# Order of the last two gate blocks in a half, three small jobs on other engines, and two queue intervals, in a two-layer hybrid encoder

## The chip, the cores and the metric

The kernel runs on one core of one Trainium2 chip. The metric is the time of one execution on the device in microseconds (us). A core has five engines with an instruction stream each: TensorE (PE in the profile; its weight loads are PEld) multiplies matrices into PSUM, VectorE (DVE), ScalarE (ACT) and GpSimd (POOL) do elementwise work, and SyncE (SP) issues DMAs. Each engine takes its instructions in order, so that an instruction that waits holds up all that stand behind it on its engine.

## What is computed

The reference runs two layers over 2048 rows (tokens) of 1024 values in float32:

```
for l in range(DEPTH):                                 # DEPTH = 2
    h = rmsnorm(x, pre_g[l])
    proj = jnp.einsum('bsd,de->bse', h, w_in[l])
    u_a, v_a, g_a, q, k, v, g_b = jnp.split(proj, idx, axis=-1)   # 512, 512, 512, 512, 128, 128, 512
    y_a = gmlp_group(u_a, v_a, ln_a_g[l], ln_a_b[l], spatial_w[l], spatial_b[l]) * jax.nn.silu(g_a)
    y_b = gqa_axial_attention(q, k, v, q_norm_g[l], k_norm_g[l], tables) * jax.nn.silu(g_b)
    out = jnp.einsum('bse,ed->bsd', jnp.concatenate([y_a, y_b], axis=-1), w_out[l])
    x = x + rmsnorm(out, post_g[l])
```

`gmlp_group` normalises v over its channels, mixes it over the 128 rows of a chunk with one 128x128 matrix per group of 64 channels, adds a bias per row, and multiplies by u. `gqa_axial_attention` has 8 query heads and 2 key/value heads of 64, with normalised and rotated q and k, and attends over all 2048 rows.

## The kernel before

**Number format.** Most products are made in three passes of a high and a low part (`PASSES`: high times high, high times low, low times high). A weight block of 256 columns is loaded as `w_raw` (`load_w`), and `split_w` makes `w_hi` (a ScalarE copy, L267) and `w_lo` (a VectorE subtraction, L268) from it. Seven buffers hold such blocks.

**Projections.** `Project.run` handles the 2048 rows in two halves, each of two groups of 512 rows. A group's rows are loaded (`x_t`), normalised (squares on ScalarE, a reciprocal root in eight small VectorE steps, and a scaling by `g_row` on VectorE, L299), transposed on TensorE, and stored as high and low part `hT` (a ScalarE copy, L309, and a VectorE subtraction, L310). `hT_jobs` returns this work as four `preps` (rows) and eight `trans` (a half row tile each). Within a half the blocks of columns come in the order k/v, q (two blocks), v of the gating part (two blocks together), attention gate (two blocks, `do_gb`), and then four gate blocks c = 0 to 3, each with 128 gate columns and 128 u columns: for each group 24 matmuls for the gate (`proj_ch`), 24 for u, and `do_gate`. In the first half, just before the product of the last gate block with the second group, the `preps` of the next half's first group are called, and its `trans` are handed to `bg`. The tiles `hT` of a group, `k_t`, `v_t` and later `wo` share six buffers ("big"), so that the next half's `hT` takes the buffers of the first group of this half when that group's last product is done.

**What sets the order.** `bg` is a list of jobs with due times, counted in ticks: `proj_ch` ticks after every 4 of its 24 matmuls, `proj_tok` after every 8, and each tick runs at most two due jobs. `bg.flush()` at the end of a half runs what is left, all at once. Instructions that are made through `PE`, `ACT`, `DVE` and `POOL` (all of TensorE's among them; they all carry line L84 in the profile) stay in the order of the program. Those made through `nc.scalar`, `nc.vector`, `nc.gpsimd` and `nc.sync` are sorted by the framework, which places an instruction where it believes its engine to be free and its inputs and buffers to be ready, sometimes far ahead of its place in the program.

**Small jobs that the change touches.** `norm_row` loads `g_row` (128x1024) and multiplies it by a constant on ScalarE (L185); layer 0 does so at the start, and for layer 1 it is called at the start of layer 0's attention. `spatial_weights` (called in the first half of each layer) transposes the eight mixing matrices, copies them from PSUM to `wsT` on VectorE (L233, two of 128x512), and makes `zbias` with eight VectorE copies of 64x128 from PSUM (L249, L250). A fill with ones of two partitions of `k_t` (2x4096 halves, L1187, VectorE) stands at the beginning of each layer; the rows are needed from the attention on.

**Attention.** `attend` makes 32 units (4 blocks of 512 queries, 8 heads) of 16 steps, with one step k of the loop for each 128 keys: two score matmuls (`sp`), two exponentials on ScalarE, a subtraction (GpSimd, every seventh on VectorE), and the products of earlier steps (`po`, `sums`). Other work is put into the steps by number: 16 steps with the row maxima of a later unit (`pmax` on TensorE, a VectorE reduction `mx`), `max_row` (`m_neg`), and `stack_max`, which transposes `m_neg` on TensorE (`t`) and stores it for `load_q` of that unit, at step `k0 + span + 3`, two after `max_row`. The output projection of the query block before (`pout`) fills in between. The steps that follow a finished output tile (`post_steps`: eight small VectorE steps of a reciprocal root, two VectorE additions of 128x512, a store, and in layer 0 for the first eight tiles also the next layer's normalisation with two more 128x512 scalings, 24 steps in all) go to `post_queue`, of which each k takes at most two. For the last four tiles of a layer (`last=True`) `post_steps` begins with four multiplications by `g_post` of 128x256 on GpSimd (`gain`); the steps of two tiles are interleaved.

Of the kernel before, what the change touches and what calls it, by code (L numbers as in the profile page):

```python
# [14 lines left out]
ALU = mybir.AluOpType  # L15
# [4 lines left out]
P = 128  # L20
# [3 lines left out]
TPG = GRP // P  # L24
NH = 8
HD = 64
# [8 lines left out]
NORM_SCALE = -8192.0 / D ** 0.5  # L35
# [3 lines left out]
def encoder(ctx: ExitStack, tc, x, w_in, w_out, pre_g, post_g, ln_a_g, ln_a_b,  # L39
            spatial_w, spatial_b, q_norm_g, k_norm_g, rope, out):  # L40
    nc = tc.nc
# [133 lines left out]
    class Project:  # L175
# [5 lines left out]
        def norm_row(self):  # L181

            self.g_row = lay.tile([P, D], F32, name="g_row")
            nc.sync.dma_start(self.g_row, pre_g[self.l].partition_broadcast(P))
            nc.scalar.mul(self.g_row, self.g_row, 1.0 / NORM_SCALE)  # L185

# [28 lines left out]
        def spatial_weights(self):  # L215
# [5 lines left out]
            for hf in range(2):  # L221
# [6 lines left out]
                def t(hf=hf, raw=raw, hi=hi, lo=lo):  # L228
# [3 lines left out]
                    sl = slice(hf * GRP, (hf + 1) * GRP)  # L232
                    nc.vector.tensor_copy(wsT[:, sl], ps)  # L233
                    nc.scalar.copy(hi, wsT[:, sl])
# [8 lines left out]
            for c in range(4):  # L243
                def b(c=c):
# [3 lines left out]
                    PE.matmul(ps[:, 0:2 * P], ones1, sb[:, 2 * c * P:(2 * c + 2) * P], start=False, stop=True)  # L248
                    nc.vector.tensor_copy(self.zbias[0:HD, c, :], ps[0:HD, 0:P])  # L249
                    nc.vector.tensor_copy(self.zbias[HD:P, c, :], ps[HD:P, P:2 * P])  # L250
                bg.add(WS_DELAY + 8 + 2 * c, b)
# [269 lines left out]
        def run(self, kv, first, last_jobs, first_wo):  # L521
# [5 lines left out]
            for n, gs in enumerate(halves):  # L527
# [50 lines left out]
                if n + 1 < len(halves):  # L578
                    blocks.append([C_K])
                if n + 1 == len(halves):  # L580
                    self.scale_v()
                    last_jobs()
                for b in range(2):
# [5 lines left out]
                    w = w_next  # L589
                for c in range(4):  # L590
                    raw = self.load_w(blocks.pop(0)) if blocks else None
                    for i, g in enumerate(gs):
                        if i == len(gs) - 1 and c == 3 and n + 1 < len(halves):
                            g2 = halves[n + 1][0]
                            hTs[g2], preps, trans = self.hT_jobs(g2)
                            for j in range(TPG):
                                preps[j]()
                            for m, f in enumerate(trans):
                                bg.add(6 + 2 * m, f)
                        pg = self.proj_ch(hTs[g], w, 0)  # L600
                        pu = self.proj_ch(hTs[g], w, P)
                        self.do_gate(g, c, pg, pu)
                        if i == 0 and c == 3 and n + 1 == len(halves):
                            hTs[g] = None
                            first_wo()
                        if i == 0 and raw is not None:
                            w_next = self.split_w(raw)
                    w = w_next
                w_kv = w
# [19 lines left out]
    def attend(l, kv, nxt):  # L629
# [25 lines left out]
        def at(k, f):  # L655
            later.setdefault(k, []).append(f)
# [298 lines left out]
        def post_steps(s, t, last=False):  # L955
            z = small.tile([P, 1], F32, name="rs_o", bufs=4)

            def gain(i):
                sl = slice(i * WB, (i + 1) * WB)
                return lambda: POOL.tensor_tensor(s.o[:, sl], s.o[:, sl], g_post[:, sl], ALU.mult)  # L960

# [82 lines left out]
        for u in range(pre, len(units)):  # L1044
# [5 lines left out]
            at(k0 + span + 1, lambda u=u: max_row(u, DVE))  # L1050
            at(k0 + span + 3, lambda u=u: stack_max(u, PE, ACT, DVE))

# [39 lines left out]
        for k in range(end + 4):  # L1092
            if k < total:
# [11 lines left out]
                if not dve_share(k):  # L1105
                    sub_lo(k, POOL)
            for _ in range(2):
                if post_queue:
                    post_queue.pop(0)()
            kb = k - 1  # L1110
# [70 lines left out]
    for l in range(DEPTH):  # L1181
# [4 lines left out]
        kv.append(v_t.bitcast(F16)[:, 1].rearrange("p (t k d) -> p t k d", t=NT, k=NKV))  # L1186
        nc.vector.memset(kv[1][HD:HD + 2], 1.0)  # L1187
        att = attend(l, kv, layers[l + 1] if l + 1 < DEPTH else None)
# [43 lines left out]
```

## Time and profile before

| | us |
|---|---|
| median of 3 runs | 2773.86 (2772.46 to 2774.44) |
| the profiled execution: its time | 2771.47 |
| the profiled execution: span from first to last instruction | 2769.3 |
| TensorE busy | 2677.1 (97%) |
| VectorE busy | 1896.8 (68%) |
| ScalarE busy | 1522.7 (55%) |
| GpSimd busy | 1287.0 (46%) |

The first layer's projections take the first 620 us of the span or so, its attention lasts to about 1390, and the second layer follows in the same way. A row of a timeline has the start, the duration, engine, line, operation, output and inputs, shapes and a count where several of a kind follow one another; in brackets is the idle time of the engine before it, and what ended that. A row of the waits view has who waited for whom, the total in us, how many times, and the longest. A row of the windows view has a stretch and its length, the busy time of each engine with its count of instructions, then TensorE's granted clock as a share, the mean share of the DMA engines, and GB/s.

### The profile page before, as it was taken

How to read it: one execution, taken by the hardware profiler on the slowest of the kernel's cores; microseconds unless marked ns; L12 is line 12 of the kernel's file. 1: busy time of each engine (PE TensorE's matmuls, PEld its weight loads, DVE VectorE, ACT ScalarE, POOL GpSimd, SP SyncE). 2: the span in 40 equal slices, each digit the busy share in tenths (PEclk: the TensorE clock that was granted, in tenths of full speed). 3: DMA queues.
4: the chain of work that ended last, by engine and by line, in shares of the span. 5: the costliest groups of instructions: out<-in, count | busy, mean ns of one | idle time of the engine just before them, and what ended most of it. 6: DMA issues, size and time to landing. Idle time of an engine off the chain costs nothing.

```text
span 2769.3 us, 48428 instructions
## 1 busy us (share of the span) xinstructions
PE 2677.1 (97%) x18230; PEld 1782.0 (64%) x18230; DVE 1896.8 (68%) x3796; ACT 1522.7 (55%) x3005; POOL 1287.0 (46%) x1080
## 2 busy tenths in 40 slices
PE   7999999999999999999999999999999999999997
PEld 6898899764444444444589989997644444444444
DVE  8862688876666776776487528888766666666664
ACT  4221432117887787787732214221288877778774
POOL 1210122007786676776632101210277767667765
PEclk9999999999999999999999999999999999999999
DMA  4424522322222232222354334333322222221313
GB/s 143 146 81 127 165 76 81 112 63 89 89 71 81 75 98 79 82 80 80 110 179 138 115 114 134 88 92 98 94 64 72 82 70 73 81 76 47 112 46 129
DMA packets 275310, 265.31 MB, mean 96 GB/s; under 512 B 19202, under 2 KB 233346, under 8 KB 275076
## 3 DMA queue, kind: packets, MB, share of 16 engines
q1 hardware_dynamic: 275076, 262.22, 30.2%
q8 instruction: 143, 2.34, 0.3%
q14 instruction: 91, 0.75, 0.1%
HBM read 177.09 MB, written 85.07 MB: 95 GB/s over the span
## 4 chain that ended last, share of the span: by engine, by line
PE 77%; DVE 11%; ACT 5%; DMA 3%; issue 2%; POOL 1%; SPq 0%; DVEq 0%; POOLq 0%; ACTq 0%
PE pp L84 27%; PE sp L84 14%; PE po L84 11%; PE pout L84 11%; PE pmax L84 7%; PE sums L84 4%; PE pt L84 2%; DVE fc L363 2%; ACT p_parts L84 2%; ACT p_f L84 2%; DMA w_raw<-in_w_in_dram 1%; DVE mx L84 1%; DVE o_t L84 1%; DVE w_lo L268 1%; ACT w_hi L267 1%
## 5 line engine op out<-in xcount | busy, mean ns | idle before, releaser
L84 POOL TENSOR_TENSOR p_parts<-p_f,p_parts 128x512 f16<-128x512 f32 x872 | 1034.9, 1205 | 404.2 <-ACT p_f L84 304.3
L84 ACT ACTIVATE p_parts<-sp 128x512 f16<-128x512 f32 x1024 | 630.0, 615 | 296.5 <-PE sp L84 289.8
L84 DVE TENSOR_REDUCE mx<-pmax 128x1 f32<-128x512 f32 x768 | 513.0, 681 | 211.9 <-PE pmax L84 209.9
L84 PE MATMUL pout<-wo,y_t 128*128 128x512 f32 x1488 | 657.1, 506 | 0.7 <-ACT p_f L84 0.3
L84 PE MATMUL po<-p_parts,v_st 128*32 128x512 f16 (+1 forms) x3072 | 639.2, 383 | 0.2
L84 ACT ACTIVATE p_f<-sp 128x512 f32<-128x512 f32 x1024 | 632.0, 617 | 0.0
L84 PE MATMUL pp<-w_hi,hT 128*128 128x256 f32 x3584 | 502.5, 290 | 16.1 <-DVE hT L310 9.7
L84 PEld LDWEIGHTS pp<-w_hi,hT 128*128 128x128 f32 x3584 | 462.0, 194 | 21.8 <-DVE hT L310 10.9
L84 PE MATMUL sp<-q_st,k_t 128*128 128x512 f16 x1024 | 390.2, 381 | 8.3 <-DVE mx L84 5.5
L84 PE MATMUL pmax<-k_t,q_m 128*128 128x512 f16 x1024 | 389.7, 382 | 7.6 <-DVE mx L84 3.2
L84 PEld LDWEIGHTS <-v_st 128*32 128x32 f16 (+1 forms) x3072 | 193.7, 96 | 309.5 <-issue 253.0
L84 PE MATMUL sp<-q,k_t 66*128 66x512 f16 x1024 | 391.0, 382 | 0.0
L84 PEld LDWEIGHTS pout<-wo,y_t 128*128 128x128 f32 x1488 | 281.3, 190 | 128.4 <-issue 8.7
L84 PEld LDWEIGHTS <-k_t 128*128 128x128 f16 (+1 forms) x2048 | 191.5, 99 | 187.7 <-issue 74.4
L468 POOL TENSOR_TENSOR fl<-fa,fh 128x512 fp32r<-128x512 f32 x32 | 43.1, 1346 | 533.3 <-ACT fh L467 489.2
L84 PE MATMUL pp<-hT,w_hi 128*128 128x512 f32 x1024 | 271.7, 413 | 0.0
L84 PE MATMUL pp<-w_lo,hT 128*128 128x256 f32 x1792 | 262.6, 290 | 0.0
L84 PE MATMUL sums<-p_parts,one_h 128*32 128x512 f16 x2048 | 242.3, 380 | 0.0
L84 PEld LDWEIGHTS pp<-w_lo,hT 128*128 128x128 f32 x1792 | 235.5, 194 | 0.9
L84 PEld LDWEIGHTS pp<-hT,w_hi 128*128 128x128 f32 x1024 | 193.4, 190 | 35.3
L683 DVE TENSOR_REDUCE mx<-pmax 128x1 f32<-128x512 f32 x256 | 172.6, 687 | 49.1 <-PE pmax L84 47.5
L84 PEld LDWEIGHTS <-q_m 128*128 128x128 f16 x1024 | 99.8, 98 | 140.2 <-issue 42.1
(161 smaller groups left out, 2790.9 us busy)
## 6 DMA issues: line engine op xcount, KB each, us to landing
w_raw<-in_w_in_dram SPq DMA_DIRECT2D x28, 1024.0 KB
y_t<-y_d SPq DMA_DIRECT2D x56, 512.0 KB
w_raw<-in_w_in_dram SPq DMA_DIRECT2D x32, 512.0 KB
x_t<-in_x_dram SPq DMA_DIRECT2D x16, 512.0 KB
z_d<-fb SPq DMA_DIRECT2D x32, 256.0 KB
gb_d<-fa SPq DMA_DIRECT2D x32, 256.0 KB
fb<-z_d SPq DMA_DIRECT2D x32, 256.0 KB
y_d<-fh SPq DMA_DIRECT2D x32, 256.0 KB
```

The costliest lines, as they stand in the source:

```text
L84: return tc.keep_in_program_order(call(*args, **kw))
L267: nc.scalar.copy(hi[:, sl], raw[:, sl])
L268: nc.vector.tensor_tensor(lo[:, sl], raw[:, sl], hi.bitcast(F32)[:, sl], ALU.subtract)
L363: nc.vector.tensor_tensor(t2[:, :, :, lo:lo + 16], qn[:, :, :, hi:hi + 16], tbi[:, :, 1:2, lo:lo + 16].broadcast_to([P, 2, n, 16]), ALU.mult)
L468: nc.gpsimd.tensor_tensor(lo, th, hi.bitcast(F32), ALU.subtract)
L683: dve.tensor_reduce(s.mx[:, j, c:c + 1], ps, AX.X, ALU.max)
```

## The change

- In the first half of each layer, gate blocks 2 and 3 are made group by group: (block 2, group 0), (3, 0), (2, 1), (3, 1) in place of (2, 0), (2, 1), (3, 0), (3, 1). The `preps` and `trans` of the next half are started ahead of (2, 1), which is two products of a block with a group ahead of the end in place of one. Block 3 is split one product earlier. In both halves the next weight block is loaded right after the split of the one before.
- `g_row` is scaled on GpSimd in place of ScalarE.
- `wsT` and `zbias` are copied from PSUM by ScalarE in place of VectorE.
- The fill of ones is made by GpSimd in place of VectorE, and stands in the last half of each layer, ahead of `scale_v`.
- `gain` of the last tile of the last layer runs on VectorE in place of GpSimd.
- `stack_max` comes two steps later, and `post_queue` gives one piece per step in place of two.

```diff
-            nc.scalar.mul(self.g_row, self.g_row, 1.0 / NORM_SCALE)
+            nc.gpsimd.tensor_scalar(self.g_row, self.g_row, 1.0 / NORM_SCALE, None, ALU.mult)
...
-                    nc.vector.tensor_copy(wsT[:, sl], ps)
+                    nc.scalar.copy(wsT[:, sl], ps)
...
-                    nc.vector.tensor_copy(self.zbias[0:HD, c, :], ps[0:HD, 0:P])
-                    nc.vector.tensor_copy(self.zbias[HD:P, c, :], ps[HD:P, P:2 * P])
+                    nc.scalar.copy(self.zbias[0:HD, c, :], ps[0:HD, 0:P])
+                    nc.scalar.copy(self.zbias[HD:P, c, :], ps[HD:P, P:2 * P])
...
                 if n + 1 == len(halves):
+                    nc.gpsimd.memset(self.kv[1][HD:HD + 2], 1.0)
                     self.scale_v()
...
-                for c in range(4):
-                    raw = self.load_w(blocks.pop(0)) if blocks else None
-                    for i, g in enumerate(gs):
-                        if i == len(gs) - 1 and c == 3 and n + 1 < len(halves):
-                            g2 = halves[n + 1][0]
-                            hTs[g2], preps, trans = self.hT_jobs(g2)
-                            for j in range(TPG):
-                                preps[j]()
-                            for m, f in enumerate(trans):
-                                bg.add(6 + 2 * m, f)
-                        pg = self.proj_ch(hTs[g], w, 0)
-                        pu = self.proj_ch(hTs[g], w, P)
-                        self.do_gate(g, c, pg, pu)
...
-                        if i == 0 and raw is not None:
-                            w_next = self.split_w(raw)
-                    w = w_next
+                more = n + 1 < len(halves)
+                order = [(c, i) for c in range(4) for i in range(len(gs))]
+                if more:
+                    order[-2 * len(gs):] = [(c, i) for i in range(len(gs)) for c in (2, 3)]
+                parts, raw = {0: w}, self.load_w(blocks.pop(0))
+                for m, (c, i) in enumerate(order):
+                    g = gs[i]
+                    if more and (c, i) == (2, len(gs) - 1):
+                        g2 = halves[n + 1][0]
+                        hTs[g2], preps, trans = self.hT_jobs(g2)
+                        for j in range(TPG):
+                            preps[j]()
+                        for j, f in enumerate(trans):
+                            bg.add(6 + 2 * j, f)
+                    pg = self.proj_ch(hTs[g], parts[c], 0)
+                    pu = self.proj_ch(hTs[g], parts[c], P)
+                    self.do_gate(g, c, pg, pu)
...
+                    split = (len(parts) - 1) * len(gs)
+                    if more and len(parts) == 3:
+                        split -= 1
+                    if raw is not None and m >= split:
+                        parts[len(parts)] = self.split_w(raw)
+                        raw = self.load_w(blocks.pop(0)) if blocks else None
...
-                return lambda: POOL.tensor_tensor(s.o[:, sl], s.o[:, sl], g_post[:, sl], ALU.mult)
+                engine = DVE if nxt is None and t == NT - 1 else POOL
+                return lambda: engine.tensor_tensor(s.o[:, sl], s.o[:, sl], g_post[:, sl], ALU.mult)
...
-            at(k0 + span + 3, lambda u=u: stack_max(u, PE, ACT, DVE))
+            at(k0 + span + 5, lambda u=u: stack_max(u, PE, ACT, DVE))
...
-            for _ in range(2):
-                if post_queue:
-                    post_queue.pop(0)()
+            if post_queue:
+                post_queue.pop(0)()
...
-        nc.vector.memset(kv[1][HD:HD + 2], 1.0)
```

More of the change, by code (lines that the diff above doesn't have):

```diff
@@ L589, in run @@
                     w = w_next
-                for c in range(4):
-                    raw = self.load_w(blocks.pop(0)) if blocks else None
-                    for i, g in enumerate(gs):
-                        if i == len(gs) - 1 and c == 3 and n + 1 < len(halves):
-                            g2 = halves[n + 1][0]
-                            hTs[g2], preps, trans = self.hT_jobs(g2)
-                            for j in range(TPG):
-                                preps[j]()
-                            for m, f in enumerate(trans):
-                                bg.add(6 + 2 * m, f)
-                        pg = self.proj_ch(hTs[g], w, 0)
-                        pu = self.proj_ch(hTs[g], w, P)
-                        self.do_gate(g, c, pg, pu)
-                        if i == 0 and c == 3 and n + 1 == len(halves):
-                            hTs[g] = None
-                            first_wo()
-                        if i == 0 and raw is not None:
-                            w_next = self.split_w(raw)
-                    w = w_next
+                more = n + 1 < len(halves)
@@ new lines, in run @@
+                order = [(c, i) for c in range(4) for i in range(len(gs))]
[14 more added lines that the diff above has]
+                    self.do_gate(g, c, pg, pu)
+                    if not more and (c, i) == (3, 0):
+                        hTs[g] = None
+                        first_wo()
+                    split = (len(parts) - 1) * len(gs)
[4 more added lines that the diff above has]
+                        raw = self.load_w(blocks.pop(0)) if blocks else None
@@ L609, in run @@
+                w = parts[max(parts)]
                 w_kv = w
```

## The prediction

> **What bounds the kernel now.** I read the page first, then TensorE's waits, then short windows around the longest of them.
>
> ```profile
> span 2769.3 us, 48428 instructions
> ...
> PE 2677.1 (97%) x18230; PEld 1782.0 (64%) x18230; DVE 1896.8 (68%) x3796; ACT 1522.7 (55%) x3005; POOL 1287.0 (46%) x1080
> ```
>
> TensorE is busy for 2677.1 of 2769.3 us. The change leaves its matmuls as they are, so all that can be gained lies in its 92.2 idle us, and in time when it is busy but slow. Its waits, in the waits view of TensorE alone, name the places:
>
> ```profile
> PE pp L84 <- DVE hT L310: 9.7, 5, 4.6
> PE t L84 <- DVE m_neg L84: 6.3, 9, 1.1
> PE sp L84 <- DVE mx L84: 5.5, 6, 1.9
> PE pp L84 <- DVE zbias L250: 4.5, 2, 2.5
> PE pt L84 <- DVE hT L84: 4.5, 1, 4.5
> PE pt L84 <- DVE fc L365: 3.9, 4, 3.0
> PE pmax L84 <- DVE mx L84: 3.2, 3, 1.5
> ```
>
> These seven end on VectorE, each at a small job, and the change touches all but `fc`. Windows add a second cost:
>
> ```profile
> 123.20:126.50 3.30, 3.27 (x15) 3.30 (x16) 3.21 (x7) 0.00 (x0) 1.39 (x1) 0.50 0.99 353
> 320.00:330.00 10.00, 10.00 (x86) 10.00 (x85) 10.00 (x38) 4.79 (x15) 1.98 (x2) 1.00 0.68 221
> 956.00:959.40 3.40, 3.40 (x23) 1.24 (x25) 3.26 (x12) 2.35 (x5) 1.69 (x2) 0.50 0.20 81
> 1150.60:1153.90 3.30, 3.30 (x19) 1.22 (x22) 3.19 (x11) 2.32 (x5) 2.96 (x3) 0.50 0.20 81
> 1405.10:1409.90 4.80, 4.77 (x23) 4.77 (x24) 4.80 (x12) 0.59 (x1) 2.32 (x3) 0.50 0.14 47
> 1693.40:1696.60 3.20, 3.20 (x17) 3.20 (x16) 3.20 (x16) 2.62 (x8) 0.00 (x0) 0.50 0.92 307
> ```
>
> The third number from the end is the granted clock. Right behind five of the longest stalls TensorE runs for 3 to 5 us at 0.50: 15 matmuls in 3.30 us at 123, against 86 in 10 us at 320. Half of such a window is lost on top of the stall, yet it counts as busy.
>
> **Part by part.** The sum is made against the profiled execution's 2771.47 us (2.2 around its span), which is 2.4 under the median of 2773.86.
>
> *Order of the gate blocks.*
>
> ```profile
> 290.00:302.00 12.00, 12.00 (x55) 9.94 (x54) 7.33 (x16) 7.87 (x19) 1.50 (x1) 1.00 0.40 103
> 302.00:314.00 12.00, 12.00 (x61) 9.94 (x60) 11.54 (x35) 3.90 (x8) 1.29 (x1) 1.00 0.51 160
> 345.00:390.00 45.00, 44.27 (x371) 43.99 (x370) 38.94 (x96) 15.79 (x35) 9.60 (x9) 1.00 0.27 82
> ```
>
> ```profile
> 314.32 0.69 DVE L310 TENSOR_TENSOR hT<-pt,hT 128x512 fp32r<-128x512 f32 x1 [0.46 <-ACT hT L309]
> ...
> 314.85 2.35 PE L84 MATMUL pt<-ident,x_t 128*128 128x128 f32 x20
> 319.32 1.22 PE L84 MATMUL pp<-w_hi,hT 128*128 128x256 f32 x8 [2.13 <-DVE hT L310]
> ...
> 1691.69 1.22 PE L84 MATMUL pp<-w_hi,hT 128*128 128x256 f32 x8 [2.13 <-DVE hT L310]
> ```
>
> In a window's row VectorE is the third of the busy times (those with x and a count). A block has 48 matmuls and so 12 ticks; the eight transposes are due at ticks 6 to 20, so that three run in the last block and five (20 matmuls, 2.35 us) in the flush, whose evacuations TensorE then waits for: 2.13 us in each layer. Two blocks have 24 ticks. The buffers of `hT` come free when the first group's last product is done, which now is two products ahead of the end, so all eight can run within the products. Is there room on VectorE? In the last two blocks it is busy for 7.33 + 11.54 = 18.9 of 24 us; the five evacuations of the flush add 5 x 0.69 = 3.5. It fits, if barely. What moves with the rows: their four loads on SP's queue, ahead of the loads and stores of one more gate block, which they would hold up only if a row buffer were missing; there are five, and the gate blocks use none. The earlier weight split and load keep within seven buffers: two blocks in use, one block being split, one raw. Gain 2 x 2.13 = 4.3, and half of the clock window at 1693, 1.6: 5.9. I take 2.1 of it back: in layer 0 VectorE is busy 38.94 of 45 us behind this place, and ends a wait of 3.0 us for `fc` there (waits view); when TensorE comes 2.1 us earlier, it may wait that much longer. Taken -3.8; bounds 0 (evacuations still late) and -9 (`fc` earlier too).
>
> *Copies of `wsT` and `zbias` to ScalarE.*
>
> ```profile
> 120.81 0.58 ACT L410 CAST fh<-pt 128x512 f16<-128x512 f32 x1 [1.93 <-PE pt L84]
> ...
> 122.79 0.29 DVE L250 COPY zbias<-pt 64x128 f32<-64x128 f32 x1
> ```
>
> The waits view has two stalls of `pp` behind `zbias`, 4.5 us in all, the longest 2.5: the product waits for a PSUM bank that `zbias` holds in VectorE's queue (the last copy at 122.79), while ScalarE sits idle (1.93 us before 120.81). A ScalarE conversion of 512 columns takes 0.58 us; a copy of 128 columns should take no more than that, against 0.29 us on VectorE. It may stand behind such a conversion, so I leave 0.5 us of each stall: 4.5 - 1.0, and half of the window at 123, 1.6: -5.1. Bounds: 0 (ScalarE itself waits) and -6.1. The two copies of `wsT` I count at nothing: they fall into the same ScalarE idle time; without it they would cost some 0.6 us each.
>
> *The last tile's `gain` on VectorE.*
>
> ```profile
> 2741.39 0.42 DVE L84 TENSOR_TENSOR gb<-gb,rden 128x256 f32<-128x256 f32 x1
> ...
> 2751.56 12.10 POOL L84 TENSOR_TENSOR o_t<-o_t,g_post 128x256 f32<-128x256 f32 x15 [0.62 <-ACT pout L84]
> ...
> 2763.28 2.92 DVE L84 SCALAR_TENSOR_TENSOR o_t<-o_t,rs_o,x_w 128x512 f32<-128x512 f32 x4
> ```
>
> GpSimd's fifteen take 0.81 us each and end at 2763.66, but only the last addition (of four in the 2.92 us from 2763.28) needs its last result. VectorE's rows have no idle time ahead of them (no bracket), so four more instructions of 0.42 us lengthen the end: +1.7 (bounds -1 and +3).
>
> *Fill of ones, and `g_row` on GpSimd.*
>
> ```profile
> 21.93 3.47 DVE L1187 MEMSET k_t<- 2x4096 f16 x1 [0.91 <-issue]
> ...
> 336.91 1.06 ACT L185 ACTIVATE g_row<-g_row 128x1024 f32<-128x1024 f32 x1 [6.23 <-DMA g_row<-in_pre_g_dram]
> ...
> 1400.88 3.47 DVE L1187 MEMSET k_t<- 2x4096 f16 x1 [0.91 <-issue]
> ```
>
> The fill stands between VectorE and the evacuation that TensorE waits for. At 1400 its 3.47 us go from the 4.5 us stall of `pt` behind `hT L84`; the window behind shrinks from 4.8 us to perhaps one of 3.2, worth 0.8: -4.3. At 22 the fill stands ahead of the 4.6 us stall of `pp` behind `hT`, but that one also hangs on a weight load, so I take 1.5 of 3.47. GpSimd needs 3.47 us or more for the fill (unknown here), at a time of its own choice before the attention. `g_row` (1.06 us on ScalarE; on GpSimd up to 3.2, four times the 0.81 of 256 columns above) keeps its 6.23 us wait, now on GpSimd, with `fa` and `fc` products queued behind; GpSimd is 46% busy and TensorE works through that stretch. Taken 0; bounds -1 and +3 (GpSimd late for the rotation). Together -5.8, from 0 to -9.
>
> *`stack_max` two steps later* removes the waits on `m_neg`: of 6.3 us I take 5.5. The stored maxima are then due one step ahead of `load_q` for the last unit, ten steps before use: no cost. Bounds 0 and -6.3.
>
> *`post_queue` at one per step.*
>
> ```profile
> 951.51 3.03 DVE L84 SCALAR_TENSOR_TENSOR o_t<-o_t,rs_o,x_r 128x512 f32<-128x512 f32 x2
> ```
>
> Two additions in one step hold VectorE for 3.03 us, the maxima behind them keep their PSUM banks, and TensorE stops (up to 1.9 us in the waits view). With one per step a reduction gets between. Such waits sum to 5.5 + 3.2 = 8.7; I take two thirds, 5.8, since the additions still follow in neighbouring steps, and both windows (956 and 1150), 3.3: -9.1. A tile's 24 pieces take 24 steps in place of 12; tiles follow in about 26 (52 entries at two per step), so buffers are back in time, if barely. Bounds 0 and -12.
>
> Sum: -3.8 - 5.1 + 1.7 - 5.8 - 5.5 - 9.1 = -27.6; 2771.5 - 27.6 = 2743.9, and with 2.4 to the median 2746.3.
>
> **The rivals.**
>
> *The half-speed windows stay.* If they are not the stalls' doing, all my clock terms (1.6 + 1.6 + 0.8 + 3.3 = 7.3) fall away: 2753.6. For it: the 2.13 us stall before 319.32 has none behind it (1.00 from 320 to 330). Against it: five begin within 2 us of a stall. [...]
>
> *The waits move on.* TensorE arrives earlier, and VectorE, the end of these seven waits, is late at the next place (38.94 of 45 us busy from 345 to 390; two additions in neighbouring steps still 3 us). Then half is kept: 2773.9 - 14 = 2760.
>
> *Slower: an in-order queue takes up a wait it did not have.* All projection work but TensorE's is sorted anew, and GpSimd now holds `g_row`'s 6.23 us, ScalarE copies that wait for TensorE. If a rotation or a weight split stands behind, TensorE waits up to 6.2 + 3.2 = 9.4, of which I put 8, with 1.6 of clock: nearly 10 in each of four halves, 38 in all against 28: 2784 (2773.9 + 38 - 28). It decides where the consumer follows within 8 us; GpSimd's idle 54% speaks against.
>
> *Nothing:* moved work is as late as before, and parts cancel: within 0.2%, 5.5 us, which is about what a measurement can tell from no change.
>
> **How the numbers follow.** Forecast 0.55, windows stay 0.14, waits move on 0.17: faster 0.86. Nothing 0.07, slower 0.07. The time is the forecast's, 2746.3. Low end: all terms near their bounds, -9 - 6.1 + 1.7 - 9 - 6.3 - 12 = -40.7, is 2733. High end: the waits-move-on case with a third kept in place of half, 2773.9 - 9 = 2765. Left out: nothing, slower, and some of the edges.
>
> **What would show it.** Right: no wait of `pp` for `hT` at the two changes of half, and no 20 transposes in a row; `zbias` and `L1187` gone from VectorE; the transition at 1400 with a stall near 1 us; no `t` waiting for `m_neg`; no pair of additions of 3 us, and 1.00 where it was 0.50; TensorE's idle time near 92 - 20 us; four more `gain` on VectorE in the tail, and its last addition 1 to 2 us further from TensorE's last matmul. Wrong: TensorE's idle time above 85 us, new waits on GpSimd or ScalarE among the first ten, or the same windows at 0.50.

## The result and the profile after

| | before | after |
|---|---|---|
| median, us | 2773.16 (2770.9 to 2774.44, 4 runs) | 2743.64 (2742.76 to 2744.58, 4 runs) |
| ratio | | 0.9894, 95% interval 0.9877 to 0.9912 |
| the profiled execution: its time | 2771.47 | 2743.25 |
| its span | 2769.3 | 2741.4 |

The changed kernel is 29.5 us faster by the medians and 27.9 by the spans. The head of its page:

```profile
span 2741.4 us, 48436 instructions
...
PE 2668.4 (97%) x18230; PEld 1776.3 (65%) x18230; DVE 1856.9 (68%) x3778; ACT 1524.4 (56%) x3023; POOL 1298.3 (47%) x1080
```

TensorE has the same 18230 matmuls and is busy 8.7 us less (2677.1 to 2668.4). Nearly all of that is clock: ahead of its last matmul it ran 30.7 us at 0.50 before and 13.7 after, and half of the difference is 8.5. Its idle time went from 92.2 to 73.0, 19.2 less. The two make up the 27.9.

To see where, take the same matmul in both traces and subtract the starts:

| place | after minus before, us |
|---|---|
| layer 0: middle of the first half's products | -6.7 |
| layer 0: first product of the second half | -8.8 |
| layer 0: a quarter into the second half | -11.1 |
| layer 0: end of the products | -11.3 |
| layer 1: first product | -19.5 |
| layer 1: middle of the first half's products | -22.8 |
| layer 1: first product of the second half | -24.9 |
| layer 1: end of the products | -25.8 |
| last matmul | -29.1 |
| end of the span | -27.9 |

TensorE's waits after (who for whom, total us, times, longest):

```profile
PE pmax L84 <- DVE mx L84: 7.3, 11, 2.3
PE pp L84 <- DVE hT L310: 4.6, 1, 4.6
PE pt L84 <- DVE fc L365: 4.1, 4, 2.4
PE pp L84 <- ACT hT L309: 3.0, 1, 3.0
```

Of the seven rows of before, `zbias`, `m_neg` and the 4.5 us of `pt` for `hT` L84 are gone, and `pp` for `hT` L310 has one wait left of five, the one at the start. But `pmax` for `mx` grew from 3.2 to 7.3, and the wait for ScalarE's `hT` from 0.7 to 3.0, into the first ten. The prediction named a new wait on ScalarE among the first ten as a sign of being wrong; the run with `g_row` back on ScalarE, below, shows why this one costs nothing. The longest wait of all, for the first rows at the start (`x_t`), which the prediction leaves out, went from 12.7 to 10.5. The windows view at or near the five places that the prediction names as half speed (the clock is third from the end):

```profile
120.40:123.60 3.20, 3.20 (x23) 2.73 (x23) 2.34 (x5) 0.00 (x0) 2.22 (x2) 1.00 0.96 325
968.20:971.40 3.20, 3.20 (x32) 1.12 (x24) 0.69 (x2) 0.00 (x0) 0.43 (x1) 0.50 0.42 153
1136.00:1139.00 3.00, 3.00 (x34) 1.44 (x36) 3.00 (x5) 2.65 (x6) 2.47 (x3) 1.00 0.00 0
1384.80:1387.80 3.00, 2.88 (x14) 2.48 (x13) 2.88 (x5) 3.00 (x8) 3.00 (x5) 0.50 0.96 292
1670.00:1673.00 3.00, 3.00 (x28) 3.00 (x27) 3.00 (x12) 1.99 (x6) 1.18 (x1) 1.00 0.15 58
```

Three run at full clock. In the first attention one half-clock window is left, at another stall, and the transition at 1384 has one of 3.4 us where before had 6.8 in a row. Two more half-clock stretches, behind the stall of the start and behind the wait for `fc` (at 393 before, 381 after), are in both traces. The change of half in layer 0, in the timeline of TensorE:

```profile
306.43 0.60 PE L84 MATMUL pt<-ident,x_t 128*128 128x128 f32 x4
306.79 2.09 PE L84 MATMUL pp<-hT,w_lo 128*128 128x512 f32 x8
308.71 1.98 PE L84 MATMUL pp<-hT,w_hi 128*128 128x512 f32 x8
310.53 1.12 PE L84 MATMUL pp<-w_hi,hT 128*128 128x256 f32 x8
```

The transposes (`pt`) come in fours between products, the last of them four us ahead of the next half's first product at 310.53, which has no wait (no bracket).

### The profile page after: what moved, and what is told of

Read it like the earlier page. It is cut to its first block, busy times and chain, and to the rows that moved or that the text cites. A ratio compares the mean times of both kernels' runs of the same rounds, so it can differ in the third digit from the quotient of the medians.

```text
span 2741.4 us, 48436 instructions
## 1 busy us (share of the span) xinstructions
PE 2668.4 (97%) x18230; PEld 1776.3 (65%) x18230; DVE 1856.9 (68%) x3778; ACT 1524.4 (56%) x3023; POOL 1298.3 (47%) x1080
## 4 chain that ended last, share of the span: by engine, by line
PE 82%; DVE 8%; ACT 5%; DMA 2%; issue 2%; POOL 1%; SPq 0%; DVEq 0%; POOLq 0%; ACTq 0%
PE pp L84 29%; PE sp L84 14%; PE po L84 12%; PE pout L84 11%; PE pmax L84 7%; PE sums L84 4%; PE pt L84 3%; ACT p_parts L84 2%; ACT p_f L84 1%; DVE fc L363 1%; DMA w_raw<-in_w_in_dram 1%; DVE mx L84 1%; DVE w_lo L268 1%; DVE p_parts L84 1%; DVE o_t L84 1%
## 5 line engine op out<-in xcount | busy, mean ns | idle before, releaser
L84 POOL TENSOR_TENSOR p_parts<-p_f,p_parts 128x512 f16<-128x512 f32 x872 | 1037.4, 1208 | 396.9 <-ACT p_f L84 293.6
L84 ACT ACTIVATE p_parts<-sp 128x512 f16<-128x512 f32 x1024 | 627.2, 612 | 297.1 <-PE sp L84 289.9
L84 DVE TENSOR_REDUCE mx<-pmax 128x1 f32<-128x512 f32 x768 | 510.8, 680 | 232.7 <-PE pmax L84 230.7
L84 PE MATMUL pout<-wo,y_t 128*128 128x512 f32 x1488 | 655.6, 505 | 1.0 <-ACT p_f L84 0.7
L84 PE MATMUL po<-p_parts,v_st 128*32 128x512 f16 (+1 forms) x3072 | 638.9, 383 | 0.2
L84 ACT ACTIVATE p_f<-sp 128x512 f32<-128x512 f32 x1024 | 628.0, 613 | 0.4 <-DVE p_parts L84 0.4
L84 PE MATMUL pp<-w_hi,hT 128*128 128x256 f32 x3584 | 499.0, 288 | 9.0 <-DVE hT L310 4.6
L84 PEld LDWEIGHTS pp<-w_hi,hT 128*128 128x128 f32 x3584 | 459.1, 193 | 13.5 <-DVE hT L310 4.8
L84 PE MATMUL pmax<-k_t,q_m 128*128 128x512 f16 x1024 | 388.9, 381 | 12.7 <-DVE mx L84 7.3
L84 PE MATMUL sp<-q_st,k_t 128*128 128x512 f16 x1024 | 389.2, 380 | 5.1 <-ACT p_f L84 2.8
L84 PEld LDWEIGHTS <-v_st 128*32 128x32 f16 (+1 forms) x3072 | 193.5, 96 | 308.9 <-issue 252.1
L84 PE MATMUL sp<-q,k_t 66*128 66x512 f16 x1024 | 390.1, 381 | 0.0
L84 PEld LDWEIGHTS pout<-wo,y_t 128*128 128x128 f32 x1488 | 280.7, 190 | 134.3 <-issue 15.1
L84 PEld LDWEIGHTS <-k_t 128*128 128x128 f16 (+1 forms) x2048 | 191.3, 98 | 184.4 <-issue 71.5
L84 PE MATMUL pp<-hT,w_hi 128*128 128x512 f32 x1024 | 273.1, 413 | 0.0
L84 PE MATMUL pp<-w_lo,hT 128*128 128x256 f32 x1792 | 260.1, 288 | 0.0
L84 PE MATMUL sums<-p_parts,one_h 128*32 128x512 f16 x2048 | 243.3, 381 | 0.0
L84 PEld LDWEIGHTS pp<-w_lo,hT 128*128 128x128 f32 x1792 | 232.9, 192 | 1.0
L84 PEld LDWEIGHTS pp<-hT,w_hi 128*128 128x128 f32 x1024 | 192.8, 189 | 35.2
L84 PEld LDWEIGHTS <-q_m 128*128 128x128 f16 x1024 | 99.8, 98 | 143.0 <-issue 41.6
```

What stands on the lines that cost most here:

```text
L84: return tc.keep_in_program_order(call(*args, **kw))
```

## The experiments

Theory A: the parts act each at its own place, so that their gains add; most of a gain is a wait of TensorE plus half of the half-clock window that it starts. Theory B: the parts hang together, or waits that one removes come back at the next place. Times are medians beside the kernel before on the same chip. Two traces differ by a half-clock window or two even in a stage that both kernels leave alone: the first attention took 766.9 us before, with two such windows, and 764.2 to 764.4 with none in the traces of the first three runs here. So the medians carry the verdicts and the traces the places.

**The order of the gate blocks alone** (before, with the change's new loop over the four gate blocks, its earlier weight loads among it, and nothing else):

```
+                    order[-2 * len(gs):] = [(c, i) for i in range(len(gs)) for c in (2, 3)]
...
+                    if more and (c, i) == (2, len(gs) - 1):
```

> The kernel before with the new order of the gate blocks alone. Theory A (the parts add up: each removes the wait at its own place, and the half-speed window behind it): both 2.13 us stalls at the change of half go, as in the changed kernel, the window at 1693 goes, and VectorE's relief behind the change of half gives some more; 6 to 9 us faster, near 2765. Theory B (the parts depend on each other, since a wait that goes only brings TensorE earlier to the next late VectorE): most is given back within the next 100 us, by a longer wait for fc; 0 to 3 us faster, near 2772.

2764.88 against 2772.86: ratio 0.9969 (0.9957 to 0.998), 8.0 us less. In its trace the waits of `pp` for `hT` L310 fall from 9.7 to 5.5, all at the start. (Its trace is that of its slowest execution, 4.4 us shorter than before's.)

**The copies of `wsT` and `zbias` on ScalarE alone:**

```
-                    nc.vector.tensor_copy(wsT[:, sl], ps)
+                    nc.scalar.copy(wsT[:, sl], ps)
...
-                    nc.vector.tensor_copy(self.zbias[0:HD, c, :], ps[0:HD, 0:P])
+                    nc.scalar.copy(self.zbias[0:HD, c, :], ps[0:HD, 0:P])
```

> The kernel before with the copies of wsT and zbias on ScalarE alone. Theory A: both stalls behind zbias (2.47 and 2.04 us) and the window at 123 go, 6 to 7 us faster, near 2767. Theory B: TensorE waits for ScalarE or the next VectorE result in their place, 0 to 3 us faster, near 2772.

2764.10: ratio 0.9969 (0.9957 to 0.998), 8.8 us less. No wait for `zbias` is left in the trace; a copy takes 0.26 us on ScalarE.

**The fill on GpSimd alone, later in the program:**

```
-        nc.vector.memset(kv[1][HD:HD + 2], 1.0)
...
+                    nc.gpsimd.memset(self.kv[1][HD:HD + 2], 1.0)
                     self.scale_v()
```

> The kernel before with the fill of ones on GpSimd, late, alone. Theory A: the 4.49 us stall at 1400 shrinks to 1 us and half of the 6.8 us window behind it goes; at the start the 4.57 us stall stays about as long, because other VectorE work steps into the gap, as in the changed kernel; 4 to 6 us faster, near 2769. Theory B: the evacuations at 1400 wait for something else, 0 to 2 us faster.

2763.97: ratio 0.9967 (0.9954 to 0.998), 8.9 us less, more than either theory said. At the transition the 4.49 us stall is down to 0.5, and the stall of the start is shorter by 1.9 (TensorE's timeline of this kernel, beside 4.57 before):

```profile
28.59 2.83 PE L84 MATMUL pp<-w_hi,hT 128*128 128x256 f32 x12 [2.64 <-DVE hT L310]
```

The fill did not come late, though: GpSimd runs it at 31.9 and 1401.2 us, near the start of each layer, where the framework sorted it. What counts is that it left VectorE.

**`stack_max` two steps later alone:**

```
-            at(k0 + span + 3, lambda u=u: stack_max(u, PE, ACT, DVE))
+            at(k0 + span + 5, lambda u=u: stack_max(u, PE, ACT, DVE))
```

> The kernel before with stack_max two steps later alone. Theory A: the waits of t for m_neg (6.3 us) go, 5 to 6 us faster, near 2768. Theory B: in the attention TensorE runs ahead of VectorE only to wait at the next reduction, so that removed waits come back on pmax and sp; the two attention stages of the changed kernel gained 7.8 us together where 14.6 were forecast, and this part is the one that gives nothing: 0 to 2 us faster, near 2773.

2770.34: ratio 0.9994 (0.9984 to 1.0003), 2.5 us less, which can't be told from nothing. TensorE's waits in its trace have no `m_neg`, but:

```profile
PE pmax L84 <- DVE mx L84: 7.0, 9, 1.5
PE sp L84 <- DVE mx L84: 4.8, 5, 1.9
PE sp L84 <- ACT p_f L84: 2.9, 6, 1.4
```

The 6.3 us for `m_neg` are gone and `pmax` waits 7.0 for `mx` where it waited 3.2, `sp` 2.9 for ScalarE where it waited 1.0. VectorE is behind at these steps, and the next instruction of TensorE that needs it shows the same lag. This is Theory B, inside one part.

**One piece of `post_queue` per step alone:**

```
-            for _ in range(2):
-                if post_queue:
-                    post_queue.pop(0)()
+            if post_queue:
+                post_queue.pop(0)()
```

> The kernel before with one piece of the post queue per step in place of two, alone. In the changed kernel the two attention stages gained 7.8 us together. Theory A (stack_max gives its 5.5): this part is worth only 2 to 3 us, because the additions still meet other VectorE work, and waits of pmax for mx come back elsewhere; near 2771. Theory B (stack_max gives nothing, because its waits come back): this part gives all of it, 7 to 9 us, near 2766, with both windows at 956 and 1150 gone.

2767.04 against 2773.53: ratio 0.9974 (0.9962 to 0.9985), 6.5 us less, between the two theories. In its waits the mirror image of the run before:

```profile
PE t L84 <- DVE m_neg L84: 9.3, 11, 1.3
...
PE pmax L84 <- DVE mx L84: 2.5, 2, 2.2
```

The waits for `mx` fall from 8.7 to about 3, and those for `m_neg` rise from 6.3 to 9.3. The half-clock windows at 956 and 1150 are not there, and one at 979 is new.

**The last tile's `gain` back on GpSimd** (the kernel after without this part):

```
-                engine = DVE if nxt is None and t == NT - 1 else POOL
-                return lambda: engine.tensor_tensor(s.o[:, sl], s.o[:, sl], g_post[:, sl], ALU.mult)
+                return lambda: POOL.tensor_tensor(s.o[:, sl], s.o[:, sl], g_post[:, sl], ALU.mult)
```

> The changed kernel with the last tile's multiplications by g_post back on GpSimd. Theory A (VectorE is the end of the path there, GpSimd is not): the tail behind TensorE's last matmul is 15.9 us again in place of 17.1, 1.2 us faster than the changed kernel, near 2742.4. Theory B (GpSimd slows VectorE's additions in the tail, so that its four multiplications cost as much there): the same as the changed kernel, 2743.6, or slower.

2741.71: ratio 0.9882 (0.9868 to 0.9897), 1.9 under the kernel after by medians; the intervals overlap, but the stretch behind TensorE's last matmul, 17.1 us after, is 15.9 in this trace as in every other without the part but one: 17.0 in that of `post_queue` alone, where VectorE's steps are the same and the span ends 4.2 us behind its last addition in place of 3.1. VectorE's tail after:

```profile
2727.18 4.76 DVE L84 SCALAR_TENSOR_TENSOR o_t<-o_t,rs_o,x_w 128x512 f32<-128x512 f32 x4
2731.87 1.42 DVE L84 TENSOR_TENSOR o_t<-o_t,g_post 128x256 f32<-128x256 f32 x4
...
2735.52 2.74 DVE L84 SCALAR_TENSOR_TENSOR o_t<-o_t,rs_o,x_w 128x512 f32<-128x512 f32 x4
```

and with `gain` on GpSimd:

```profile
2725.69 4.76 DVE L84 SCALAR_TENSOR_TENSOR o_t<-o_t,rs_o,x_w 128x512 f32<-128x512 f32 x4
...
2732.69 2.92 DVE L84 SCALAR_TENSOR_TENSOR o_t<-o_t,rs_o,x_w 128x512 f32<-128x512 f32 x4
```

The four multiplications add 1.42 us to a chain without gaps, and shorten the last four additions by 0.18.

**`g_row` back on ScalarE** (the kernel after without this part):

```
-            nc.gpsimd.tensor_scalar(self.g_row, self.g_row, 1.0 / NORM_SCALE, None, ALU.mult)
+            nc.scalar.mul(self.g_row, self.g_row, 1.0 / NORM_SCALE)
```

> The changed kernel with the scaling of g_row back on ScalarE. In the changed kernel GpSimd takes 2.77 us for it and TensorE starts 2.2 us earlier, but then waits 3.0 us for the hT copy behind ScalarE's weight conversion. Theory A: the start gains nothing from it, and near 330 the 6.2 us wait of ScalarE comes back: 0 to 1 us slower than the changed kernel, 2744. Theory B (ScalarE's wait near 330 holds up hT copies and through them TensorE): 2 to 4 us slower, 2747.

2742.30: ratio 0.9886 (0.987 to 0.9903), 1.3 under the kernel after, where both theories had it the same or slower; the intervals can't tell it from the same time. What the move does at the start is in the timelines. After:

```profile
6.91 2.77 POOL L185 TENSOR_SCALAR g_row<-g_row 128x1024 f32<-128x1024 f32 x1 [5.61 <-DMA g_row<-in_pre_g_dram]
...
15.47 2.32 PE L84 MATMUL pp<-w_hi,hT 128*128 128x256 f32 x8 [2.99 <-ACT hT L309]
...
27.19 1.41 DVE L299 SCALAR_TENSOR_TENSOR x_t<-x_t,rs_x,g_row 128x512 f32<-128x512 f32 x2
28.52 1.88 DVE L310 TENSOR_TENSOR hT<-pt,hT 128x512 fp32r<-128x512 f32 x3
...
29.25 2.76 PE L84 MATMUL pp<-w_hi,hT 128*128 128x256 f32 x12 [4.64 <-DVE hT L310]
```

With `g_row` on ScalarE:

```profile
27.84 0.68 DVE L310 TENSOR_TENSOR hT<-pt,hT 128x512 fp32r<-128x512 f32 x1
...
28.58 2.73 PE L84 MATMUL pp<-w_hi,hT 128*128 128x256 f32 x12 [2.64 <-DVE hT L310]
```

After, the scaling of two half rows (27.19, 1.41 us) has stepped ahead of the evacuation that TensorE waits for; with `g_row` on ScalarE the evacuation comes first. The length of this stall differs from trace to trace (2.64 to 4.24 us in the six with the fill on GpSimd and `g_row` on ScalarE), as VectorE's first weight split there (`w_lo`, L268) waits for ScalarE's `w_hi` and starts at 24.7 to 26.3 us. But from the start of that split to the end of the stall it is 3.4 us in all six, and 5.3 in the three with `g_row` on GpSimd (after, `gain` back, the ladder): the order costs 1.8. So the move gives back at the start a part of what the fill had freed. The 2.99 us wait at 15.47 costs nothing: TensorE began its transposes 2.4 us earlier than with ScalarE and then waited for the same `hT`.

**A ladder of stalls** (the kernel after, with 16 more reductions of 256 to 4096 elements on VectorE in each attention, whose results nothing else uses, each followed by a transpose on TensorE that must wait for it; nothing is left out, and the time only tells of the added stalls):

```
+        def stall(n):
+            DVE.tensor_reduce(scr[:, 0:1], k_st.rearrange("p k s -> p (k s)")[:, 0:256 * (n + 1)], AX.X, ALU.max)
+            ps = ps_t("t3")
+            PE.transpose(ps[0:32, 0:P], scr, ident)
```

> The changed kernel with 16 added VectorE reductions of 256 to 4096 elements in each layer's attention, 19 steps apart, each followed by a small TensorE transpose that waits for it: stalls of TensorE from about 0 to 5 us, whose results nothing uses. Window theory: the clock is set on a fixed grid of 3.41 us (all half-speed windows of the two kernels begin on one grid), by how long TensorE was idle in the grid window before; from about 1.8 us of idle time in one grid window the next runs at 0.50, so that a stall of 2 us costs its length alone or 1.7 more, depending on where it falls; stalls under 1.7 us never bring one. [...] Chance theory: windows do not follow the stalls. Time lost: the stalls, plus 1.7 for each window, perhaps 50 to 100 us in all.

2909.6 in a single run, 166 us over the kernel after where 50 to 100 were expected: TensorE is idle 115.8 us more and busy 50.3 more. In the trace of before, and in that of after, the half-clock windows begin whole multiples of 3.41 us apart, on a grid that lies differently in each: an edge is 0.2 us behind the first instruction before, and 2.2 after. The windows at 0.50 below are whole multiples of 3.41 us apart too. The windows view of this kernel, each pair a grid window and the one behind it:

```profile
1159.49:1162.90 3.41, 1.65 (x8) 0.62 (x6) 2.49 (x4) 2.75 (x6) 3.41 (x4) 1.00 0.92 281
1162.90:1166.31 3.41, 1.83 (x9) 1.01 (x10) 2.81 (x5) 0.88 (x2) 0.42 (x1) 1.00 0.81 239
2620.40:2623.81 3.41, 1.56 (x8) 0.83 (x9) 3.05 (x4) 0.35 (x1) 0.38 (x1) 1.00 0.67 231
2623.81:2627.22 3.41, 3.41 (x17) 1.52 (x16) 2.36 (x4) 3.35 (x8) 1.53 (x2) 1.00 0.00 0
951.28:954.69 3.41, 1.61 (x8) 0.51 (x6) 2.19 (x6) 3.41 (x9) 2.85 (x3) 1.00 0.01 2
954.69:958.10 3.41, 2.49 (x10) 1.66 (x10) 1.71 (x4) 0.04 (x1) 1.15 (x1) 0.50 0.00 0
2330.27:2333.68 3.41, 1.43 (x8) 0.83 (x8) 2.06 (x7) 1.17 (x3) 1.16 (x1) 1.00 0.00 0
2333.68:2337.09 3.41, 3.41 (x9) 1.48 (x8) 1.34 (x3) 2.04 (x4) 1.15 (x1) 0.50 0.00 0
```

Idle time of TensorE is the length less its busy time, the first with a count: 1.76 us in the first pair, and the next window runs at 1.00; 1.85 and 1.00; 1.80 and 0.50; 1.98 and 0.50. Over all grid windows that ran at 1.00 in the traces of before and after (from where the record of the clock begins, 20.7 us into the span before and 19.2 after), 1.70 us or less of idle time was never followed by 0.50, 2.28 or more always was, and between them it went both ways: 1.80 was followed by 1.00 (at 1495 before), 1.86, 1.90 and 1.91 (before) and 1.79 (after) by 0.50. A place in the trace of the next run does not fit (1.53 us idle, then 0.50), so that idle time alone does not decide every case:

```profile
1384.77:1388.18 3.41, 1.88 (x13) 1.47 (x14) 2.95 (x11) 3.20 (x8) 3.41 (x6) 1.00 0.88 294
1388.18:1391.59 3.41, 3.41 (x18) 3.41 (x18) 3.41 (x9) 1.40 (x3) 3.41 (x6) 0.50 0.93 309
```

The two changes of half before, in the same view:

```profile
317.68:321.09 3.41, 1.77 (x14) 1.77 (x15) 3.41 (x7) 3.41 (x11) 1.29 (x1) 1.00 1.03 381
...
1689.84:1693.25 3.41, 1.55 (x13) 1.56 (x14) 3.41 (x8) 3.41 (x12) 1.30 (x1) 1.00 0.99 305
1693.25:1696.66 3.41, 3.41 (x19) 3.41 (x18) 3.41 (x16) 2.77 (x9) 0.00 (x0) 0.50 0.91 304
```

The same stall of 2.13 us lay across the edge of two grid windows in layer 0, with 1.64 in the second, and no half clock followed; in layer 1 1.86 fell into one window, and half clock followed. So the length of a stall alone does not tell whether half clock follows. The traces of the copies, the fill, `stack_max` and `post_queue` alone have the same stall of 2.13 us in both layers: with those of before, four of ten such stalls were followed by half clock.

**Both costly parts out: `gain` on GpSimd and `g_row` on ScalarE** (the two diffs above together):

> The kernel after with both operations of the change that cost time alone put back: the last tile's gain on GpSimd (1.9 us less when done alone) and the scaling of `g_row` on ScalarE (1.3 us less alone). Theory A (the parts add, each at its own place): 1.9 + 1.3 = 3.2 us below the kernel after, about 2740.4, 30 to 35 us under the kernel before. Theory B (parts stand in each other's way): no better than the better of the two alone, about 2742.

2740.91 against 2774.56: ratio 0.9877 (0.986 to 0.9893), 33.7 us under before, against 31.8 and 31.2 with one of them: what adding says, though the intervals don't exclude that it is the better of the two.

**Weighted `post_queue`, two small pieces a step** (on the kernel of the run before; `add` and `scale` carry `f.heavy = True`):

```
-            if post_queue:
-                post_queue.pop(0)()
+            for n in range(2):
+                heavy = post_queue and getattr(post_queue[0], "heavy", False)
+                if post_queue and not (heavy and (n or 0 <= k - 1 < total and dve_share(k - 1))):
+                    post_queue.pop(0)()
+                if heavy:
+                    break
```

> The kernel of the run before, with the rest of the output rows handed out by weight: one of the 128x512 operations on VectorE (`add`, `scale`) alone in a step, and in no step in which VectorE makes a score tile's subtraction; of the small pieces two in a step, as before the change. If the reading holds that only the 128x512 pieces made the waits for `mx`, the waits for `mx` and `m_neg` in attention are no longer than in the kernel after (about 8 us), and the small pieces two by two cost nothing: the time is that of the run before, or up to 5 us less by waits and half-clock windows that go. If the count of pieces per step is what matters, the `mx` waits come back in part: 3 to 6 us more than the run before.

2740.65: ratio 0.988 (0.9865 to 0.9895), no different from the run before. The waits for `mx` are 9.8 us in its trace and 7.9 in that of the run before: not the weight of the pieces alone makes them.

**The same rule, one small piece a step** (`range(1)`):

> As the second of these four, but the small pieces one in a step, as in the kernel after: only the rule stands that a 128x512 piece is not handed out in a step in which VectorE makes a score tile's subtraction. If the weight of the pieces is what makes the waits, the time is at or up to 3 us under the first of these four; and against the second it tells whether small pieces two by two cost anything: no difference by the weight reading, 3 to 6 us less than the second by the count reading.

2738.99: ratio 0.9875 (0.986 to 0.989), the lowest median of all, 35.6 us under before where the change gave 29.5; its interval overlaps those of its neighbours and that of the change.

**`stack_max` back at three steps** (on the kernel with both costly parts out):

> The first kernel of these four with `stack_max` back at three steps after the last score matmul of its unit, where the kernel before had it. If the later `stack_max` is worth what it gave alone, the time is 2.5 us more (0 to 5). If it only shows the same lag of VectorE to the next instruction of TensorE, the waits for `m_neg` come back (some 6 to 9 us in all), those for `mx` get less by nearly as much, and the time is the same within 2 us.

2742.57: ratio 0.9885 (0.9871 to 0.99), 1.7 more by medians, not separable. In its trace the waits for `m_neg` are back with 9.3 us, and those for `mx` fall from 7.9 to 3.1: 4.5 us more in all.

The traces see more: in the second attention none of them has a half-clock window, so that its length, from the end of the last projection product to the last matmul, compares without that noise. The windows view over that stretch (the length is the second number). Before:

```profile
1996.02:2753.40 757.38, 744.88 (x5080) 358.12 (x5078) 474.45 (x819) 588.27 (x1173) 538.65 (x456) 1.00 0.24 78
```

`stack_max` alone (two pieces a step, no rule for heavy ones):

```profile
1995.14:2751.78 756.64, 744.80 (x5081) 358.13 (x5078) 471.11 (x819) 587.42 (x1172) 538.11 (x456) 1.00 0.25 78
```

Weighted, two small pieces a step:

```profile
1966.56:2722.78 756.22, 745.01 (x5080) 358.13 (x5078) 467.36 (x819) 587.42 (x1173) 540.08 (x456) 1.00 0.25 79
```

Both costly parts out (one piece a step, no rule):

```profile
1972.77:2726.78 754.01, 744.59 (x5081) 358.29 (x5078) 463.57 (x819) 587.11 (x1172) 537.62 (x456) 1.00 0.25 79
```

Weighted, one small piece a step:

```profile
1969.17:2723.17 754.00, 744.64 (x5080) 358.27 (x5078) 464.38 (x819) 587.02 (x1172) 538.31 (x456) 1.00 0.25 79
```

`stack_max` back, one piece a step:

```profile
1967.92:2723.11 755.19, 744.45 (x5081) 357.87 (x5078) 466.51 (x819) 588.08 (x1172) 539.35 (x456) 1.00 0.25 79
```

Against 757.38, `stack_max` alone gives 0.7 us, one piece per step without it 2.2 (755.19; 755.33 in the run with `post_queue` alone), both 3.4 (754.01): they help each other a little. With the later `stack_max` in all four, two pieces a step take 756.64 and 756.22, one piece 754.01 and 754.00, so that here the count of pieces matters and the rule for heavy ones does not. In the first attention, where the first eight tiles have twice as many of them, the traces of the weighted kernels have 1.6 (two pieces) and 1.5 us (one) less idle time than that without the rule, and no half-clock window where that one has one; that is a single trace each.

## Why the prediction was right, and where it was not

The sum was right within 3 us, by terms that were too small in the projections and too large in attention. By the table of places the projections and the transition gave 21.3 us where the terms sum to 14.7, and the two attentions 7.8 where they sum to 14.6. That these two errors cancel is luck. Measured alone, the parts give 8.0 + 8.8 + 8.9 + 2.5 + 6.5 = 34.7 less; with 1.9 and 1.3 for `gain` and `g_row` that is 31.5, and together they gave 29.5. So they add within their intervals, Theory A. A stall that goes at a place is not met again in another stage: up to the last matmul, no row of the table is smaller than the one above it.

**Order of gate blocks** (forecast -3.8, alone -8.0, interval of the ratio 5.5 to 11.9 us): the mechanism held, both waits of 2.13 went (8.8 - 6.7 = 2.1 in layer 0, 24.9 - 22.8 = 2.1 in layer 1), and so did the window at 1693 (1.6 more by a quarter into that half). What failed is the step "I take 2.1 of it back": the wait for `fc` in layer 0 did not grow, its longest went from 3.0 to 2.4, and TensorE gained another 2.3 us in that quarter (8.8 to 11.1, and as much with this part alone) in place of losing 2.1. Before, TensorE was idle for 1.5 us in that quarter, in three waits for VectorE (0.35 and 0.63 for `hT`, 0.49 for `fc`); after, and with this part alone, it has none there. That VectorE came out of the change of half with less work waiting would explain it; no run here separates it. Without the deduction the term is -5.9, inside the interval.

**Copies to ScalarE** (forecast -5.1, alone -8.8, 5.5 to 11.9): the 0.5 left of each stall was not needed, since a copy took 0.26 us on ScalarE, less than the 0.29 on VectorE; the bound of -6.1 is inside the interval. In its trace 5.2 us were gone by the middle of layer 0's first half and 2.3 in that of layer 1, 7.5 in all.

**Fill and `g_row`** (forecast -5.8 together; the fill alone -8.9, 5.5 to 12.8; `g_row` +1.3): the fill term was near for the transition (4.3 forecast; 3.7 of the 8.2 us between the end of layer 0's products and the first product of layer 1 fell there; a stall of 1.79 for `pout` and one half-clock window are left). The term that was mis-sized is the start: 1.5 of 3.47 forecast, 1.9 of stall and 3.7 by a quarter of the first half in the fill's own trace. Against the trace of before, the five traces with the fill on VectorE are 0 to 1.7 us later at that quarter (0.7 in the mean, before among them), the six with the fill on GpSimd and `g_row` on ScalarE 1.8 to 4.1 earlier (3.1), and the three with both on GpSimd 0.8 to 2.9 earlier (2.0): 3.8 for the fill at the start, and 1.1 lost again with `g_row`. "Taken 0" for `g_row` failed by that much there, and by 1.3 in the median, which alone could be noise. The cause is not that of its bound of +3, GpSimd late for the rotation (layer 1's `g_row`, at 332 us, waited 0.34 and took 2.78), but VectorE's sorted order at the start, which put a scaling ahead of an evacuation.

**`gain` on VectorE** (forecast +1.7): right; 1.9 by medians, 1.2 in the trace.

**`stack_max`** (forecast -5.5, alone -2.5 at most) and **`post_queue`** (forecast -9.1, alone -6.5): here the step failed that counted waits of one row as time to be had. The traces of before, after and these two parts have 15.0, 7.9, 11.8 and 12.4 us of waits for `mx` and `m_neg` together: either part alone takes 3, not 6 to 9. The rival "the waits move on" was the truth in this stage, within a step or two. Both parts together take 7.1, more than the 5.8 of the two alone. The prediction's other sign, no pair of additions of 3 us, held in part: one of 2.98 us is left at 1323.6. The two windows at 956 and 1150 did go, but the 3.3 us for them can't be credited to this part: the traces of the first three runs have none there either, with nearly the same waits in attention (15.0 to 15.2 us for `mx` and `m_neg`). And one came at another stall, at 968, which the timeline of after shows:

```profile
963.58 1.35 DVE L84 SCALAR_TENSOR_TENSOR x_r<-o_t,rs_o,g_row 128x512 f32<-128x512 f32 x1
...
964.87 1.64 DVE L84 TENSOR_TENSOR p_parts<-p_f,p_parts 128x512 f16<-128x512 f32 x1
...
967.15 0.38 PE L84 MATMUL pmax<-k_t,q_m 128*128 128x512 f16 x1 [2.28 <-DVE mx L84]
```

A scaling of 1.35 us is now followed by the subtraction of 1.64, which falls to VectorE in every seventh step, and the reduction for TensorE stands behind both. So the attention term of 14.6 came to 4.5 us in layer 0 (the other part of 8.2, above) and 3.3 in layer 1, 7.8. Where no trace has a half-clock window (764.3 us for the first attention as it was, 760.5 and 760.8 in the two runs that took back `g_row` or `gain`; 757.4 and 754.1 for the second) it is 3.6 and 3.3.

**The clock.** The rival "windows stay" was wrong: where a stall went, as at 123 and 1693, so did its 0.50. Half of a window was near the price of a window that occurs (1.6 us at 1693, 2.6 for the two of the first attention), but the stall alone does not tell whether one occurs (of the two stalls of 2.13 us before, the one with 1.86 in one grid window had it behind it and the one with 1.64 had not), so that the terms of 1.6 and 3.3 priced a draw as a certainty. The copies alone still had the 1.9 us stall of the first attention, and its windows view shows 0.35 us idle in one grid window, 1.55 in the next, and full clock behind:

```profile
945.71:949.12 3.41, 3.06 (x14) 1.29 (x13) 3.34 (x6) 2.44 (x7) 3.41 (x3) 1.00 0.00 0
949.12:952.53 3.41, 1.86 (x9) 0.87 (x8) 3.17 (x8) 3.41 (x9) 2.19 (x3) 1.00 0.37 154
952.54:955.94 3.40, 3.40 (x48) 1.52 (x48) 3.29 (x9) 1.77 (x5) 1.62 (x2) 1.00 0.00 0
```

TensorE's idle time, forecast "near 92 - 20 us", is 73.0.

**Open:** medians and traces of a part alone don't always agree: the copies gave 8.8 us where the stalls and windows in the trace explain 7.5, and the order 8.0 where its trace is 4.4 shorter. The intervals are 6 to 7 us wide, and no run here narrows them.

## What to carry to other kernels

When a wait of the busiest engine is to be removed, ask whether the engine that it waits for gets less to do ahead of that point, or whether only the place of the wait moves; `stack_max` alone moved it and gave next to nothing, the fill and the copies took work away and gave all of theirs. Sum the waits of all rows that end on one engine in one stage, not of one row. A half-clock window behind a stall in one trace is a draw: price it by how often such stalls have one, here four times in ten for the stalls of 2.13 us. And where the framework sorts the order, moving a small operation to an idle engine can let another operation step into the gap, so look at what now stands ahead of the instruction that is waited for.

## What the runs showed of the hardware

In the traces of before and after, TensorE's half-clock windows begin whole multiples of 3.41 us apart; the grid's first edge is 0.2 us behind the first instruction before and 2.2 after. TensorE idle for 2.28 us or more within one grid window at full clock was followed by 0.50 in the next in these two traces, 1.70 or less by 1.00, and 1.79 to 1.91 by either. In the ladder's rows 1.76 and 1.85 were followed by 1.00, 1.80 and 1.98 by 0.50; in the trace with both costly parts out, 1.53 was followed by 0.50. Before, the stall of 2.13 us was followed by a half-clock window in layer 1 (at 1693.25) and by none in layer 0.

GpSimd took 3.50 us for the fill (after) that took VectorE 3.47 (before), but 2.77 for the scaling of `g_row` (after) that took ScalarE 1.06 (before). In the tail of after, VectorE's additions of 128x512 took 1.19 us each (4.76 for the four from 2727.18) while GpSimd's multiplications ran, to 2731.39, and 0.69 each (2.74 for the four from 2735.52) after they had ended.
